# Six gate blocks of each MLP from seven block products, with a re-normed input and later splits

## The chip, the core and the metric

The kernel runs on one core of one Trainium2 chip. It is one program of five engines that run side by side and meet at semaphores: TensorE (PE in the profile; its weight loads are listed apart as PEld), VectorE (DVE), ScalarE (ACT), GpSimd (POOL) and SyncE (SP), which issues most of the DMAs. Operands live in SBUF and products are summed in PSUM, in banks of 128 partitions x 512 fp32. The metric is the device time of one execution in microseconds (us). The computation is in fp32, and every large matmul is made in parts, as told below.

## The reference

Two layers of a decoder trunk on 512 tokens (`S`), width 1024. Each layer has a mixer (attention and a short convolution in layer 0, gated linear attention in layer 1), the gated MLP that is changed here, and a per-layer embedding. The MLP:

```python
def _conv_ffn(h, w_up, conv_w, conv_b, w_down):
    u = _causal_depthwise_conv(h @ w_up, conv_w) + conv_b      # width 3, per column
    gate, up = jnp.split(u, 2, axis=-1)                        # 2816 columns each
    return (jax.nn.gelu(gate, approximate=False) * up) @ w_down
# in the trunk, for each layer i:
x = x + _conv_ffn(_rms_norm(x, ffn_norm[i]), ffn_w_up[i], ffn_conv_w[i], ffn_conv_b[i], ffn_w_down[i])
```

`_rms_norm` divides each token by the root of its mean square and multiplies by a gain per channel.

## The kernel before, in words

**Numbers.** An fp32 value is held as two fp32r parts, a high one and a low one (high: ScalarE rounds, L101 or L137; low: VectorE subtracts, L102 or L138). One product of two such pairs is three matmuls, `mm3` (L157 to L159): high x high, high x low, low x high. `split` makes the parts of an activation and `cut` (called by `weights`, after a DMA by SP into `raw`) those of a weight block, in two halves of 1024 elements a partition. `raw` has 2 buffers, `wh` and `wl` have 3 each.

**Layout.** The activations stand with channels in partitions and tokens in the free dimension: `xT[m]`, m = 0..7, are 128 channels x 512 tokens; `xg[m]` is the pair of parts of `xT[m]` times the gain, in the pools `a0` and `a1`. Weights are the stationary operand, 128 x 128 at a time.

**Up-projection (`ffn`).** A loop over d = 0..10 takes 256 columns of the gate and the 256 columns of the value that go with them; I call one turn a *pair* d. Each has two gate columns and two value columns of 128, in the order gate 0, value 0, gate 1, value 1. A column is 8 channel blocks (`ND`) x 3 = 24 matmuls of 512 tokens into one PSUM bank (`ps`, 4 banks; a second pool `pa` has 4 more). Behind each column stands `taps`: the sums are multiplied by `R`, the tokens' inverse root mean square spread over all partitions (L785, VectorE; the norm's factor is thus put behind the matmul), then the causal convolution: one tap with the bias on ScalarE (L786), two taps on VectorE (L788). The gate goes through Gelu (ScalarE, L810), the product of gate and value is made on VectorE (L813), and is split at once into `acts[f]`: the first 8 of the 22 into the pools `b0` and `b1` (8 buffers each), the others into tiles `four` (7 buffers).

**Down-projection.** `project` multiplies the 22 `acts` with `ffn_w_down`. In layer 0 the next norm follows, in layer 1 the seven-product embedding (`ple1`): it already replaces eight half-size block products by seven; its matmuls are recorded at L945 to L947 and are 512 wide, a few 256 wide. The gated linear attention of layer 1 has the lines L1344 (a matmul into one half of a `pa` tile) and L1351 (a copy out of the other half).

**Order.** A scheduler places the instructions of each engine; inside `manual_schedule` blocks the order of the engines named there is that of the program. A tile's buffer is used again when its readers are done, and an instruction waits for a whole tile, not for the part of it that it touches.

Of the kernel before, what the change touches and what calls it, by code (L numbers as in the profile page):

```python
# [18 lines left out]
P = 128  # L19
S = 512  # L20
D = 1024
NT = S // P
ND = D // P
DFF = 2816
NF = DFF // P
# [3 lines left out]
ET = mybir.EngineType  # L29
LEVELS = (64, 32, 16, 8, 4, 2, 1)  # L30
CW = 512
TWO_PI = 2.0 * np.pi
# [24 lines left out]
class Kernel:  # L57
# [711 lines left out]

    def ffn(self, i, next_gain):  # L770
        nc, a, tc = self.nc, self.a, self.tc
        xg, R = self.xg, None
        wu = a["ffn_w_up"][i].rearrange("(k p) n -> p k n", p=P)
        w0, w1, w2, bb = self.fcv
        with tc.tile_pool(name=f"ffn{i}", bufs=1) as fp:
            acts = [self.pair(self.fp, "b0", "b1") for f in range(8)]
            for f in range(8, NF, 2):
                four = self.four(fp)
                acts += [(four[:, 0], four[:, 1]), (four[:, 2], four[:, 3])]

            def taps(ps, f):
                y = fp.tile([P, S], F32, tag="zt", name=self.nm("zt"), bufs=4)
                z = fp.tile([P, S + 2], F32, tag="z", name=self.nm("z"), bufs=3)
                nc.gpsimd.memset(z[:, :2], 0.0)
                nc.vector.tensor_tensor(z[:, 2:], ps, R, ALU.mult)  # L785
                nc.scalar.activation(y, z[:, 2:], AF.Identity, scale=w2[:, f : f + 1], bias=bb[:, f : f + 1])  # L786
                for tap, w in ((1, w1), (0, w0)):
                    nc.vector.scalar_tensor_tensor(  # L788
                        out=y, in0=z[:, tap : tap + S], scalar=w[:, f : f + 1], in1=y, op0=ALU.mult, op1=ALU.add
                    )  # L790
                return y

            for d in range(NF // 2):
                wg = self.weights(wu[:, :, 256 * d : 256 * d + 256], ND, 256)
                wv = self.weights(wu[:, :, DFF + 256 * d : DFF + 256 * d + 256], ND, 256)
                for c in range(2):
                    f = 2 * d + c
                    got = []
                    pss = []
                    for w in (wg, wv):  # L800
                        ps = self.ps()
                        for k in range(ND):
                            self.mm3(ps, w(k, c * P, (c + 1) * P), xg[k], start=k == 0, stop=k == ND - 1)
                        pss.append(ps)
                    if R is None:
                        R = self.spread()
                    for w, ps, fo in ((wg, pss[0], f), (wv, pss[1], NF + f)):
                        y = taps(ps, fo)
                        if w is wg:
                            nc.scalar.activation(y, y, AF.Gelu)  # L810
                        got.append(y)
                    g, y = got
                    nc.vector.tensor_tensor(y, g, y, ALU.mult)  # L813
                    self.split(acts[f], y)
            self.begin_norm(("a0", "a1"))
            done = self.residual(next_gain)
            if i == 1:
                self.forms = []
                scratch = lambda: fp.tile([P, S], F32, tag="zt", name=self.nm("gx"), bufs=4)

                def done(m, ps):
                    nc.vector.tensor_tensor(self.xT[m], self.xT[m], ps, ALU.add)
                    self.blocks(m, next_gain, scratch)
# [75 lines left out]
    def ple1(self, fp):  # L899
# [49 lines left out]
        def back(hf, t):  # L949
# [6 lines left out]
            x = fp.tile([P, 512], F32, tag="zt", name=self.nm("xt"), bufs=4)  # L956
# [576 lines left out]
```

## Time and profile before

| | |
|---|---|
| time, median of 3 runs (lowest to highest) | 1247.71 us (1247.56 to 1248.11) |
| the profiled execution | 1248.2 us, of which its span in the trace is 1246.4 us |
| instructions | 15216 |
| TensorE / its weight loads, busy | 1236.1 us (99%) / 1023.9 us (82%) |
| VectorE / ScalarE / GpSimd, busy | 804.6 us (65%) / 561.5 us (45%) / 52.1 us (4%) |
| granted TensorE clock | 1.0 of full speed throughout |
| HBM read / written | 114.37 MB / 2.10 MB, 93 GB/s over the span |
| DMA of one `raw` of `ffn_w_up` (1024 KB) | 5.1 us from issue to landing |

The span is cut into engines' busy time; a group of instructions is given with its source line, its engine and operation, its output and inputs, its shape, its count, its total and mean time, and the idle time of the engine just before it with the instruction that ended it. Matmuls are pipelined: one of 512 columns is listed with about 390 ns from its start to its result, and the next starts sooner than that, so the pace is read from the distance between starts. A row of a timeline has the start in us, the duration in us, the engine and the operation; a bracket at its end is a wait and its releaser.

### The profile page before, as it was taken

The numbers are of one execution on the slowest core, as the hardware profiler recorded it, in microseconds if no ns is written. First come the engines' busy times: TensorE is split into PE (matmuls) and PEld (weight loads), VectorE is DVE, ScalarE is ACT, GpSimd is POOL, SyncE is SP. The second block draws the span as 40 slices with busy tenths as digits, with TensorE's granted clock in tenths as the row PEclk, the third lists the DMA queues.
The fourth block names the chain that finished last, engine by engine and source line by source line (L and its number), as shares of the span: only waits on it lengthen the run. The fifth ranks groups of instructions, "written<-read, shape, count | busy, mean of one in ns | idle before, by whom it ended". The sixth has DMA issues, their size and how long they took to land.

```text
span 1246.4 us, 15216 instructions
## 1 busy us (share of the span) xinstructions
PE 1236.1 (99%) x5984; PEld 1023.9 (82%) x5984; DVE 804.6 (65%) x1251; ACT 561.5 (45%) x873; POOL 52.1 (4%) x152
## 2 busy tenths in 40 slices
PE   9999999999999999999999999999999999999998
PEld 8877788888888888888987878888888888888887
DVE  6886556777777633346679875557777777444495
ACT  7466344444444322234563554335444444333374
POOL 2500000000000000000100000000000000000000
PEclk9999999999999999999999999999999999999999
DMA  6222232233333232223322222332223333322411
GB/s 214 92 80 56 83 102 83 88 100 102 101 102 101 83 103 93 93 74 103 111 91 68 69 68 68 101 110 95 83 94 102 101 101 102 101 93 94 149 46 68
DMA packets 111004, 117.45 MB, mean 94 GB/s; under 512 B 2728, under 2 KB 106210, under 8 KB 110932
## 3 DMA queue, kind: packets, MB, share of 16 engines
q1 hardware_dynamic: 109568, 115.35, 28.4%
q8 instruction: 47, 0.77, 0.2%
q0 software_dynamic: 560, 0.42, 0.2%
q10 hardware_dynamic: 804, 0.70, 0.2%
q14 instruction: 25, 0.20, 0.0%
HBM read 114.37 MB, written 2.10 MB: 93 GB/s over the span
## 4 chain that ended last, share of the span: by engine, by line
PE 88%; DVE 7%; ACT 2%; issue 1%; POOL 1%; DVEq 0%; ACTq 0%; POOLq 0%
PE ps L157 26%; PE ps L158 26%; PE ps L159 26%; DVE wl L138 1%; PE ps L947 1%; PE ps L946 1%; PE ps L945 1%; PE pa L1367 1%; PE pa L1344 0%; PE pa L595 0%; PE pa L158 0%; PE pa L192 0%; PE pa L159 0%; DVE F L1228 0%; PE pa L157 0%
## 5 line engine op out<-in xcount | busy, mean ns | idle before, releaser
L137 ACT ACTIVATE wh<-raw 128x1024 fp32r<-128x1024 f32 (+4 forms) x212 | 214.2, 1012 | 333.3 <-PE ps L158 298.7
L138 DVE TENSOR_TENSOR wl<-raw,wh 128x1024 fp32r<-128x1024 f32 (+4 forms) x212 | 246.5, 1164 | 153.2 <-ACT wh L137 152.1
L157 PE MATMUL ps<-a,wh 128*128 128x512 f32 x864 | 336.9, 390 | 0.0
L158 PE MATMUL ps<-a,wh 128*128 128x512 f32 x864 | 336.6, 390 | 0.0
L159 PE MATMUL ps<-a,wl 128*128 128x512 f32 x864 | 336.3, 389 | 0.0
L158 PEld LDWEIGHTS ps<-a,wh 128*128 128x128 f32 x864 | 162.3, 188 | 34.0 <-issue 0.3
L159 PEld LDWEIGHTS ps<-a,wl 128*128 128x128 f32 x864 | 162.2, 188 | 33.9
L157 PEld LDWEIGHTS ps<-a,wh 128*128 128x128 f32 x864 | 162.2, 188 | 33.7 <-issue 0.7
L788 DVE SCALAR_TENSOR_TENSOR zt<-z,vfa,zt 128x512 f32<-128x512 f32 x176 | 131.3, 749 | 3.6 <-ACT zt L786 0.6
L157 PE MATMUL ps<-b,wh 128*128 128x512 f32 x320 | 126.0, 395 | 0.5 <-ACT b L101 0.5
L159 PE MATMUL ps<-b,wl 128*128 128x512 f32 x320 | 125.7, 393 | 0.0
L158 PE MATMUL ps<-b,wh 128*128 128x512 f32 x320 | 125.0, 391 | 0.0
L785 DVE TENSOR_TENSOR z<-ps,R 128x512 f32<-128x512 f32 x88 | 60.3, 687 | 74.7 <-PE ps L159 74.7
L157 PE MATMUL ps<-four,wh 128*128 128x512 f32 x224 | 87.1, 389 | 0.0
L158 PE MATMUL ps<-four,wh 128*128 128x512 f32 x224 | 87.1, 389 | 0.0
L159 PE MATMUL ps<-four,wl 128*128 128x512 f32 x224 | 87.1, 389 | 0.0
L786 ACT ACTIVATE zt<-z,vfb 128x512 f32<-128x512 f32 x88 | 70.9, 808 | 5.0 <-DVE z L785 3.3
L157 PEld LDWEIGHTS ps<-b,wh 128*128 128x128 f32 x320 | 60.0, 188 | 14.0 <-ACT b L101 1.3
L159 PEld LDWEIGHTS ps<-b,wl 128*128 128x128 f32 x320 | 60.1, 188 | 12.5
L158 PEld LDWEIGHTS ps<-b,wh 128*128 128x128 f32 x320 | 60.1, 188 | 12.5
L810 ACT ACTIVATE zt<-zt 128x512 f32<-128x512 f32 x44 | 27.8, 631 | 74.9 <-DVE zt L788 74.8
L101 ACT ACTIVATE four<-zt 128x512 fp32r<-128x512 f32 x28 | 17.7, 632 | 77.3 <-DVE zt L813 77.3
(359 smaller groups left out, 1555.0 us busy)
## 6 DMA issues: line engine op xcount, KB each, us to landing
raw<-in_ffn_w_up_dram SPq DMA_DIRECT2D x44, 1024.0 KB, 5.1
raw<-in_ffn_w_down_dram SPq DMA_DIRECT2D x16, 1024.0 KB, 4.7
raw<-in_hy_w_in_dram SPq DMA_DIRECT2D x8, 1024.0 KB, 5.0
raw<-in_gla_w_in_dram SPq DMA_DIRECT2D x8, 1024.0 KB, 5.3
raw<-in_ffn_w_down_dram SPq DMA_DIRECT2D x8, 768.0 KB, 4.1
raw<-in_ple_w_gate_dram SPq DMA_DIRECT2D x6, 1024.0 KB, 4.7
raw<-in_gla_w_out_dram SPq DMA_DIRECT2D x4, 1024.0 KB, 4.8
raw<-in_gla_w_in_dram SPq DMA_DIRECT2D x4, 672.0 KB, 4.0
```

The lines of the kernel that those rows point to most:

```text
L101: nc.scalar.activation(h, src, AF.Copy)
L137: nc.scalar.activation(hv, v, AF.Copy)
L138: nc.vector.tensor_tensor(lv, v, hv.bitcast(F32), ALU.subtract)
L157: mm(out, lh, rh, start=start, stop=False)
L158: mm(out, lh, rl, start=False, stop=False)
L159: mm(out, ll, rh, start=False, stop=stop)
L785: nc.vector.tensor_tensor(z[:, 2:], ps, R, ALU.mult)
L786: nc.scalar.activation(y, z[:, 2:], AF.Identity, scale=w2[:, f : f + 1], bias=bb[:, f : f + 1])
L788: nc.vector.scalar_tensor_tensor(out=y, in0=z[:, tap : tap + S], scalar=w[:, f : f + 1], in1=y, op0=ALU.mult, op1=ALU.add)
L810: nc.scalar.activation(y, y, AF.Gelu)
L945: mm(o, lh, rh, start=first and j == 0, stop=False, **kw)
L946: mm(o, lh, rl, start=False, stop=False, **kw)
```

## The change

Three things, in both layers.

**Seven products.** For pairs d = 4 to 9 (`SEVEN = (4, 10)`) the two gate columns are not made as 2 x 8 channel blocks. The 8 channel blocks are taken as 4 couples (even block, odd block), the gate's columns as left and right 128, and the tokens as left and right 256. Each couple is then a 2 x 2 by 2 x 2 block product, made with seven block products instead of eight (Winograd's form). Of the weights, `seven` takes the blocks b11, b12 (even channels), b21, b22 (odd), cuts them into parts and makes differences between them on VectorE. Of the activations, `sums` makes four combinations per couple, s1 to s4, once per layer: in pairs d = 0 to 3, from the normed x (gain and `R` applied), split into parts in `b0` and `b1`.

In order of issue on TensorE, each product 4 couples x 3 = 12 matmuls of 256 tokens, 84 in all, into three banks, W (pool `pa`), X and Y (pool `ps`), by left and right half:

| | into | weights | activations | then, on ScalarE |
|---|---|---|---|---|
| P1 | W left, new | `w1`, first 128 | `xg` even, left | copied to Y left and to X left |
| P2 | W right, new | `w13`, first 128 | s1 | copied to `more` (SBUF) |
| P3 | Y left, added | `w2` | s2 | Y left copied to X right |
| P4 | X left, added | `w1`, second 128 | `xg` odd, left | |
| P5 | X right, added | `w13`, second 128 | s3 | X right copied to Y right |
| P6 | Y left, added | `w4`, second 128 | s4 | |
| P7 | X right, added | `w4`, first 128 | `xg` odd, right | |

X is then the first gate column; the second is Y plus `more` in both halves (VectorE). `w1`, `w13`, `w2`, `w4` are four cuts of the one `raw` tile, which VectorE changes between them: `w1` is cut from the blocks as loaded (b11 is its first 128, b21 its second); two subtractions follow and `w13` is cut from what then stands in b11 and b12; a third subtraction, and `w2` is cut (512 wide, into two tiles `t2`); a fourth, and `w4` is cut from b21 and b22. (In `ffn` the names `w0`, `w1`, `w2` mean the convolution's tap weights, as before.)

**Normed x.** From pair 4 on `xg` holds the normed x: at d = 4 the eight pairs are allocated anew in `a0` and `a1` and split from what `sums` left in `scratch`. `taps` then reads PSUM directly, with no multiplication by `R`. At d = 4 the value columns come first, at d = 5 to 9 the gate. Gelu (in pairs 4 to 9) and the product of gate and value (in all pairs) run on both columns of a pair at once, 1024 wide.

**Later splits.** The products stay in fp32 (`place`, `kept`) and are split later: the first 8 at the end of d = 9, into `b0` and `b1` (which the s1 to s4 have held until then), the others behind the loop, into `four` tiles.

The memset of two columns ahead of `z` goes with the padded form of the taps. In layer 1 the embedding takes its scratch halves from tiles of the new shape (`half`).

The diff, cut to its core:

```diff
+SEVEN = (4, 10)
+    def sums(self, j, gain, R, scratch):
+        nc = self.nc
+        H = S // 2
+        for u in range(2):
+            m = 2 * j + u
+            nc.vector.scalar_tensor_tensor(
+                out=scratch[:, u], in0=self.xT[m], scalar=gain[:, m : m + 1], in1=R, op0=ALU.mult, op1=ALU.mult
+            )
+        e, o, s12, s34 = (scratch[:, u] for u in range(4))
+        out = []
+        nc.vector.tensor_tensor(s12[:, :H], e[:, H:], o[:, H:], ALU.add)
+        nc.vector.tensor_tensor(s12[:, H:], s12[:, :H], e[:, :H], ALU.subtract)
+        nc.vector.tensor_tensor(s34[:, :H], e[:, :H], e[:, H:], ALU.subtract)
+        nc.vector.tensor_tensor(s34[:, H:], o[:, :H], s12[:, H:], ALU.subtract)
+        for x in (s12, s34):
+            hl = self.pair(self.fp, "b0", "b1")
+            self.split(hl, x)
+            for c in (slice(0, H), slice(H, S)):
+                out.append((hl[0][:, c], hl[1][:, c]))
+        return out
+    def seven(self, raw, xg, forms):
+        nc = self.nc
+        H = S // 2
+        mm = nc.tensor.matmul
+        W = self.pa()
+        X, Y = self.ps(), self.ps()
+        rv = raw.rearrange("p (j u) n -> p j u n", u=2)
+        def cut(src, wide=True):
+            if wide:
+                h, l = (self.wp.tile([P, 1024], F32R, tag=g, name=self.nm(g), bufs=3) for g in ("wh", "wl"))
+            else:
+                h, l = (self.sp.tile([P, S], F32R, tag="sq", name=self.nm("t2"), bufs=2) for _ in range(2))
+            h, l = (x.rearrange("p (j n) -> p j n", n=src.shape[2]) for x in (h, l))
+            nc.scalar.activation(h, src, AF.Copy)
+            nc.vector.tensor_tensor(l, src, h.bitcast(F32), ALU.subtract)
+            h, l = (x.rearrange("p j n -> p (j n)").rearrange("p (k n) -> p k n", n=P) for x in (h, l))
+            return lambda j, c: (h[:, (2 * j if wide else j) + c, :], l[:, (2 * j if wide else j) + c, :])
+        def product(out, w, c, x, first=False):
+            kw = dict(skip_group_check=True)
+            for j in range(ND // 2):
+                (wh, wl), (xh, xl) = w(j, c), x(j)
+                mm(out, wh, xh, start=first and j == 0, stop=False, **kw)
+                mm(out, wh, xl, start=False, stop=False, **kw)
+                mm(out, wl, xh, start=False, stop=j == ND // 2 - 1, **kw)
+        def plain(u, half):
+            c = slice(half * H, (half + 1) * H)
+            return lambda j: (xg[2 * j + u][0][:, c], xg[2 * j + u][1][:, c])
+        s1, s2, s3, s4 = (lambda j, q=q: forms[j][q] for q in range(4))
+        b11, b12, b21, b22 = (rv[:, :, u, c * P : (c + 1) * P] for u in range(2) for c in range(2))
+        left, right = slice(0, H), slice(H, S)
+        w1 = cut(raw[:, :, :P])
+        nc.vector.tensor_tensor(b11, b12, b11, ALU.subtract)
+        nc.vector.tensor_tensor(b12, b22, b12, ALU.subtract)
+        w13 = cut(rv[:, :, 0])
+        nc.vector.tensor_tensor(b11, b22, b11, ALU.subtract)
+        w2 = cut(b11, False)
+        nc.vector.tensor_tensor(b21, b21, b11, ALU.subtract)
+        w4 = cut(rv[:, :, 1])
+        with self.tc.manual_schedule(engines={ET.PE}):
+            product(W[:, left], w1, 0, plain(0, 0), True)
+            nc.scalar.copy(Y[:, left], W[:, left])
+            nc.scalar.copy(X[:, left], W[:, left])
+            product(W[:, right], w13, 0, s1, True)
+            more = self.sp.tile([P, S], F32, tag="acc", name=self.nm("more"), bufs=1)[:, :H]
+            nc.scalar.copy(more, W[:, right])
+            product(Y[:, left], w2, 0, s2)
+            nc.scalar.copy(X[:, right], Y[:, left])
+            product(X[:, left], w1, 1, plain(1, 0))
+            product(X[:, right], w13, 1, s3)
+            nc.scalar.copy(Y[:, right], X[:, right])
+            product(Y[:, left], w4, 1, s4)
+            product(X[:, right], w4, 0, plain(1, 1))
+        return X, Y, more
     def ffn(self, i, next_gain):
         nc, a, tc = self.nc, self.a, self.tc
         xg, R = self.xg, None
+        gain = self.g_ffn[i]
         wu = a["ffn_w_up"][i].rearrange("(k p) n -> p k n", p=P)
         w0, w1, w2, bb = self.fcv
         with tc.tile_pool(name=f"ffn{i}", bufs=1) as fp:
-            acts = [self.pair(self.fp, "b0", "b1") for f in range(8)]
-            for f in range(8, NF, 2):
+            forms, kept, acts = [], [], []
+            def both():
+                return fp.tile([P, 2, S], F32, tag="zt", name=self.nm("zt"), bufs=2)
+            def taps(y, ps, f, more=None, normed=True):
+                z = ps
+                if more is not None:
+                    z = fp.tile([P, S + 2], F32, tag="z", name=self.nm("z"), bufs=3)[:, :S]
+                    h2 = lambda x: x.rearrange("p (u t) -> p u t", u=2)
+                    nc.vector.tensor_tensor(
+                        h2(z), h2(ps), more.unsqueeze(1).to_broadcast([P, 2, S // 2]), ALU.add
+                    )
+                elif not normed:
+                    z = fp.tile([P, S + 2], F32, tag="z", name=self.nm("z"), bufs=3)[:, :S]
+                    nc.vector.tensor_tensor(z, ps, R, ALU.mult)
+                nc.scalar.activation(y, z, AF.Identity, scale=w2[:, f : f + 1], bias=bb[:, f : f + 1])
+                for tap, w in ((1, w1), (2, w0)):
+                    nc.vector.scalar_tensor_tensor(
+                        out=y[:, tap:], in0=z[:, : S - tap], scalar=w[:, f : f + 1], in1=y[:, tap:],
+                        op0=ALU.mult, op1=ALU.add,
+                    )
+            def columns(w, c, bank):
+                ps = bank()
+                for k in range(ND):
+                    self.mm3(ps, w(k, c * P, (c + 1) * P), xg[k], start=k == 0, stop=k == ND - 1)
+                return ps
+            def place(d):
+                if d == NF // 2 - 1:
+                    return None
+                if d % 2 == 0:
+                    kept.append(self.four(fp, F32))
+                return kept[d // 2][:, 2 * (d % 2) : 2 * (d % 2) + 2]
+            def split_pair(x):
                 four = self.four(fp)
-                acts += [(four[:, 0], four[:, 1]), (four[:, 2], four[:, 3])]
-
-            def taps(ps, f):
-                y = fp.tile([P, S], F32, tag="zt", name=self.nm("zt"), bufs=4)
-                z = fp.tile([P, S + 2], F32, tag="z", name=self.nm("z"), bufs=3)
-                nc.gpsimd.memset(z[:, :2], 0.0)
-                nc.vector.tensor_tensor(z[:, 2:], ps, R, ALU.mult)
-                nc.scalar.activation(y, z[:, 2:], AF.Identity, scale=w2[:, f : f + 1], bias=bb[:, f : f + 1])
-                for tap, w in ((1, w1), (0, w0)):
-                    nc.vector.scalar_tensor_tensor(
-                        out=y, in0=z[:, tap : tap + S], scalar=w[:, f : f + 1], in1=y, op0=ALU.mult, op1=ALU.add
-                    )
-                return y
-
+                self.split((four[:, :2], four[:, 2:]), x)
+                acts.extend([(four[:, u], four[:, 2 + u]) for u in range(2)])
+            def at(f):
+                return kept[f // 4][:, f % 4]
+            scratch = [self.four(fp, F32) for _ in range(ND // 2)]
             for d in range(NF // 2):
-                wg = self.weights(wu[:, :, 256 * d : 256 * d + 256], ND, 256)
-                wv = self.weights(wu[:, :, DFF + 256 * d : DFF + 256 * d + 256], ND, 256)
-                for c in range(2):
-                    f = 2 * d + c
-                    got = []
-                    pss = []
-                    for w in (wg, wv):
-                        ps = self.ps()
-                        for k in range(ND):
-                            self.mm3(ps, w(k, c * P, (c + 1) * P), xg[k], start=k == 0, stop=k == ND - 1)
-                        pss.append(ps)
-                    if R is None:
-                        R = self.spread()
-                    for w, ps, fo in ((wg, pss[0], f), (wv, pss[1], NF + f)):
-                        y = taps(ps, fo)
-                        if w is wg:
-                            nc.scalar.activation(y, y, AF.Gelu)
-                        got.append(y)
-                    g, y = got
-                    nc.vector.tensor_tensor(y, g, y, ALU.mult)
-                    self.split(acts[f], y)
+                g, y = both(), both()
+                normed = d >= SEVEN[0]
+                if d == SEVEN[0]:
+                    xg = []
+                    for m in range(ND):
+                        xg.append(self.pair(self.fp, "a0", "a1"))
+                        self.split(xg[m], scratch[m // 2][:, m % 2])
+                cg, cv = 256 * d, DFF + 256 * d
+                if SEVEN[0] <= d < SEVEN[1]:
+                    def value():
+                        wv = self.weights(wu[:, :, cv : cv + 256], ND, 256)
+                        for c in range(2):
+                            taps(y[:, c], columns(wv, c, self.pa), NF + 2 * d + c)
+                    def gate():
+                        raw = self.raw(ND, 256)
+                        nc.sync.dma_start(raw, wu[:, :, cg : cg + 256])
+                        X, Y, more = self.seven(raw, xg, forms)
+                        taps(g[:, 0], X, 2 * d)
+                        taps(g[:, 1], Y, 2 * d + 1, more)
+                        nc.scalar.activation(g, g, AF.Gelu)
+                    for half in (value, gate) if d == SEVEN[0] else (gate, value):
+                        half()
+                else:
+                    wg = self.weights(wu[:, :, cg : cg + 256], ND, 256)
+                    wv = self.weights(wu[:, :, cv : cv + 256], ND, 256)
+                    for c in range(2):
+                        pss = [columns(w, c, self.ps) for w in (wg, wv)]
+                        if R is None:
+                            R = self.spread()
+                        taps(g[:, c], pss[0], 2 * d + c, None, normed)
+                        nc.scalar.activation(g[:, c], g[:, c], AF.Gelu)
+                        taps(y[:, c], pss[1], NF + 2 * d + c, None, normed)
+                u = place(d)
+                if u is None:
+                    u = y
+                nc.vector.tensor_tensor(u, g, y, ALU.mult)
+                if d < ND // 2:
+                    forms.append(self.sums(d, gain, R, scratch[d]))
+                if d == SEVEN[1] - 1:
+                    for f in range(8):
+                        hl = self.pair(self.fp, "b0", "b1")
+                        self.split(hl, at(f))
+                        acts.append(hl)
+            for d in range(4, NF // 2):
+                split_pair(y if d == NF // 2 - 1 else kept[d // 2][:, 2 * (d % 2) : 2 * (d % 2) + 2])
             self.begin_norm(("a0", "a1"))
             done = self.residual(next_gain)
             if i == 1:
                 self.forms = []
-                scratch = lambda: fp.tile([P, S], F32, tag="zt", name=self.nm("gx"), bufs=4)
+                halves = []
+                def half():
+                    if not halves:
+                        x = both()
+                        halves.extend([x[:, 0], x[:, 1]])
+                    return halves.pop(0)
...
-            x = fp.tile([P, 512], F32, tag="zt", name=self.nm("xt"), bufs=4)
+            x = self.half()
```

More of the change, by code (lines that the diff above doesn't have):

```diff
@@ L818, in ffn @@
                 self.forms = []
[L819 removed]
+                halves = []
[4 more added lines that the diff above has]
+                    return halves.pop(0)
+                self.half = half
                 def done(m, ps):
                     nc.vector.tensor_tensor(self.xT[m], self.xT[m], ps, ALU.add)
[L823 removed]
+                    self.blocks(m, next_gain, half)
             self.project(self.rows(a["ffn_w_down"][i]), acts, ND, done)
```

## The prediction

> **What bounds the kernel now.** I read the page's busy shares first, then the busy time in the up-projection, its groups of instructions, and two pieces of timeline that price what the change adds.
>
> The page, parts 1 and 4:
>
> ```profile
> PE 1236.1 (99%) x5984; PEld 1023.9 (82%) x5984; DVE 804.6 (65%) x1251; ACT 561.5 (45%) x873; POOL 52.1 (4%) x152
> ...
> PE 88%; DVE 7%; ACT 2%; issue 1%; POOL 1%; DVEq 0%; ACTq 0%; POOLq 0%
> ```
>
> TensorE is the bound. The windows (span, then busy us of PE, PEld, DVE, ACT, POOL, clock, DMA share) show the first up-projection without its first two columns of output:
>
> ```profile
> 196.60:424.90 228.30, 228.30 (x1009) 189.02 (x1008) 168.68 (x213) 105.63 (x130) 4.08 (x41) 1.00 0.30 96
> ```
>
> 228.3 us for 1008 matmuls is 0.2264 each: no stall at all, so whatever TensorE is made to wait is added in full. VectorE has 60 us of 228 free. Its groups and ScalarE's in that window (mean ns before the bar's end):
>
> ```profile
> L788 DVE SCALAR_TENSOR_TENSOR zt<-z,vfa,zt 128x512 f32<-128x512 f32 x86 | 64.2, 749 | 1.8 <-ACT zt L786 0.3
> ...
> L138 DVE TENSOR_TENSOR wl<-raw,wh 128x1024 fp32r<-128x1024 f32 x42 | 51.4, 1225 | 9.2 <-ACT wh L137 8.7
> L137 ACT ACTIVATE wh<-raw 128x1024 fp32r<-128x1024 f32 x42 | 44.6, 1062 | 31.4 <-PE ps L158 31.2
> L786 ACT ACTIVATE zt<-z,vfb 128x512 f32<-128x512 f32 x43 | 34.7, 808 | 2.5 <-DVE z L785 1.7
> L785 DVE TENSOR_TENSOR z<-ps,R 128x512 f32<-128x512 f32 x43 | 29.5, 687 | 35.5 <-PE ps L159 35.5
> L813 DVE TENSOR_TENSOR zt<-zt,zt 128x512 f32<-128x512 f32 x21 | 14.5, 692 | 1.3 <-ACT zt L810 0.6
> ```
>
> The nearest rows for the new 256-column products are at the end of the second embedding (timeline of PE):
>
> ```profile
> 1239.08 0.39 PE L159 MATMUL pa<-wh,four 128*128 128x512 f32 x1
> 1239.30 0.28 PE L945 MATMUL ps<-wh,a 128*128 128x256 f32 x1
> ...
> 1242.06 0.28 PE L947 MATMUL ps<-four,b 128*128 128x256 f32 x1
> ```
>
> 24 of them stand between 1239.30 and 1242.06, so 2.76/23 = 0.120 each, 0.28 from start to result; weight loads (188 ns each) do not hold them.
>
> For a copy out of one half of a bank while the other half is wanted, the gated linear attention has the pattern:
>
> ```profile
> 752.05 0.37 ACT L1351 COPY st<-pa 128x256 f32<-128x256 f32 x1
> ...
> 752.47 0.30 PEld L1344 LDWEIGHTS pa<-vt,F 128*128 128x128 f32 x2 [0.38 <-ACT st L1351]
> ```
>
> L1351 copies one half of a `pa` tile; the matmul into its other half starts 0.05 after the copy's end. Elsewhere a restarted fp32r stream loses another 0.11 because the next weights were not loaded (gaps of 335 instead of 227 ns, at 619.05 and 1206.74).
>
> **The change, part by part.** Per gate, 48 x 0.2264 = 10.87 becomes 84 x 0.120 = 10.08: 0.79 saved, **9.4 us** for twelve gates. Everything else must hide beside that.
>
> Call the products P1 to P7 in order of issue (1.44 us each). W, X and Y are one bank each, and in the built program waits go by the whole tile. P2 (right half of W) waits for both copies of W's left half. P4 (left half of X) waits for the copy of Y into X's right half, made after P3. P6 waits for the copy of X into Y, made after P5. Bare prices: P2: 0.28 to P1's result, 0.09 to ScalarE's start (seen at L137), two copies of 0.375, 0.05 back, 0.11 restart, less the 0.12 pitch: 1.13. P4, one copy: 0.77. P6 is covered by value matmuls that the scheduler put ahead of it (five, in pairs 5 to 8), but the third of those needs the VectorE half of a weight cut whose ScalarE half may start only when P4 has read `w1`: 0.37 + 1.06 + 0.03 + 1.22 + 0.05 after P4's eleventh matmul, 0.6 to 0.7 after its turn.
>
> The Trainium skill (PSUM — Partial Sum Buffer, summary rules) says to read PSUM beside a running matmul from another bank and to guard by bank. The L1351 row agrees; if halves were free, P2 and P4 would not wait and the sum would be some 23 us less.
>
> VectorE's chain is longer still. Pairs 6 to 8, from P6's result: `more` added (0.04 + 0.69), bias step (0.84), four tap steps (3.0), next `w1` low part (1.22), two subtractions (1.38), two value taps (1.5), `w13` low part (1.22), two subtractions (1.38): 11.3. Then ScalarE: `w4` high part (1.06), the last value column's bias step (0.81), two copies (0.75), with lags 2.75: P2 can start 14.1 after P6's result. P6 to its result is 1.6, so 15.7; TensorE has only P6, P7, 43 value matmuls and P1 = 14.05 for it. P2's stall is 1.65 instead of 1.13. Pair total: 20.95 of matmuls + 1.65 + 0.77 + 0.7 + restarts 0.1 = 24.17 against 21.73 now: **+2.44 each, +7.3 for three**. The durations of steps that before doesn't show are bounded by a 512-wide copy (0.58) and a 128-wide activation (0.28) for the 256-wide copies; L1351's 0.375 has their size and source. Taps from PSUM: 0.745 at L105, as from SBUF.
>
> Pair 3 to 4: the eight normed `xg` pairs go into the buffers of the old ones, so they are cut while the last column of pair 3 runs. In the built order VectorE has in pair 3 the sums of pairs 2 and 3 (2 x 4.6), its usual 14.6 and these eight low parts (5.5) ahead of the weights of pair 4's second column: about 33 us from 21.5 before the boundary. I add them along the queue: the first `xg` low part ends 1.4 after the boundary, the eighth 10.4, the weight cut 11.6. The second column so ends at 16.75 instead of 11.1: **+5.6**.
>
> Gate 4: P2 1.15, P3 0.9 (low part of `w2` behind taps of the value columns), P4 0.78, P6 0.55 (two foreign matmuls only): 3.4 - 0.79 = **+2.6**. Pair 5's gate follows at once: P2 1.25; P3 waits for ScalarE's high part of `w2` behind the 1024-wide Gelu and then its low part behind the product, 3.4; P4 0.8; value cut 0.7: 6.2 - 0.79 = **+5.4**.
>
> Pair 9: splits of the first activations stand in ScalarE's queue between the copies, so P2 1.7, P4 1.4, P6 1.1: **+3.5** after the saving.
>
> Off the path: pairs 0 to 3 get 4.6 of sums each, 19.2 of VectorE in 21.7, four PSUM banks of slack; dropping `R` saves 28 x 0.69 of VectorE a layer; GpSimd's `z` memsets vanish; weight DMAs keep their number, 5.1 us, and are issued as buffers come free, well ahead of the cuts. The later splits (8 x 0.69 and 7 x 1.22 on VectorE, 14 a layer) lie in pairs 9 and 10, where VectorE's queue ends about 5 us ahead of each weight's use; I cost them at nothing, and at up to 14 a layer if that cover is gone.
>
> Sum per layer 13.6 + 7.3 + 3.5 = 24.4, the same order in both layers: +48.8. On the profiled execution, 1248.2 (span 1246.4, 1.8 around it): 1297.0. The median of the runs is 0.5 below the profiled one: **1296.5 us**.
>
> **Rivals.**
> - *Faster: the waits are covered and the arithmetic counts.* One mechanism: the copies run beside the other half's matmuls, and value matmuls fill the rest; then 1247.7 - 9.4 = 1238.3. It decides where a gate's stalls fall under 0.79 us. For it: VectorE and ScalarE are idle 26% and 54% of that window. Against: one copy alone costs P4 0.77, and P2 waits for two. 4%; break-even within 0.2%: 2%.
> - *Bank waits only.* VectorE's chain is absorbed: 12 x (1.13 + 0.77) + 8 x 0.7 + 2 x 5.6 - 9.4 = +30, 1278. For it: the chain misses by only half a microsecond per pair. Against: the gaps of pairs 4, 5 and 9 come from fixed queue order. 20%.
> - *Splits uncovered.* VectorE, at 17.5 of 24 us in pairs 6 to 8 and full in 3 and 9, runs late into the down-projection: +28, 1325. Against: `four` tiles are wanted only 10.9 us into it. 8%.
> - *Weight loads bound the narrow products*, so the product count doesn't fall in time: 84 x (0.188 - 0.120) = 5.7 a gate more, +69 on top: 1365. The 0.120 rows speak against it. 3%.
>
> By the Trainium skill (TensorE: Matmul & The Clock Gate, LDWEIGHTS) a load of 128 columns is estimated at 128/1.2 = 107 ns, under the 0.120 pitch.
>
> **How the numbers follow.** Forecast 63%, the rivals 4, 2, 20, 8 and 3%. Range: from 1270 (bank waits with a shorter restart) to 1314 (chain steps 10% longer, +1.5 in eight gaps, and 3 more at each boundary); it leaves out both ends' rivals, under 2 in 10. A measurement can tell about 0.2%, 2.5 us. Faster 0.04, same 0.02, slower 0.94.
>
> **What would show it.** After: 256-column matmuls at 0.120 inside a product; PE idle before P2 of 1.1 to 1.7 us put down to ScalarE's copy of W, 0.8 before P4 to the copy of Y; PE waiting for `a` tiles on VectorE at the boundary of pairs 3 and 4, some 5 us a layer; up-projections of about 261 instead of 236 us, down-projections unchanged. If P2 and P4 start without a gap, the bank reading is wrong; if the gaps of pair 6 equal those bare prices, the chain is.

## The result

The changed kernel takes 1285.32 us (median of 6; five of them between 1282.27 and 1285.53), before 1247.63 us: a ratio of 1.0295, 95% interval 1.0281 to 1.0309. Slower was forecast, 1296.5 us with a range of 1270 to 1314. The profile that came with this result is of the sixth execution, which took 2610.42 us, with 512-wide matmuls 0.45 us apart (median) instead of 0.227 at a listed clock of 1.00; the lines of the changed kernel below are from its second run, e1, whose profiled span is 1280.5 us.

The page of e1, parts 1 and 4:

```profile
PE 1240.9 (97%) x6416; PEld 1037.6 (81%) x6416; DVE 856.9 (67%) x1323; ACT 603.4 (47%) x963; POOL 44.2 (3%) x64
...
PE 71%; DVE 18%; ACT 6%; issue 3%; POOL 1%; DMA 0%; ACTq 0%; DVEq 0%; POOLq 0%
```

TensorE has 432 matmuls more (twelve gates of 84 instead of 48), and it was busy 99% of the span before; now TensorE holds 71% of the chain that ended last, where it held 88% before, and other engines hold a quarter. The windows (span, then busy us of PE, PEld, DVE, ACT, POOL, clock, DMA share, GB/s) of layer 1 from the third column of the up-projection to the first matmul with a `four` tile:

```profile
857.17:1112.68 255.51, 241.19 (x1273) 204.82 (x1272) 200.71 (x256) 129.97 (x180) 0.00 (x0) 1.00 0.28 90
```

The same stretch of before is 239.36 us long (839.30 to 1078.66), with TensorE busy in all of it. So a layer loses 16.15 us here; layer 0 loses 17.4. The down-projections behind it keep their pace: 29.92 us from one `four` group to the next, before and after. These two stretches hold 33.5 of the 34.1 us by which the spans differ.

Who TensorE waits for in that stretch of layer 1 (engine, line, waited for: us in total, times, longest). L821 to L823 are the matmuls of the products; L845 is the second copy of W, L850 that of Y into X, L853 that of X into Y, L812 and L813 the cuts in `seven`; L103 is the low part of `split`, L139 that of `cut`:

```profile
PE pa L821 <- ACT ps L845: 4.7, 6, 0.8
PE ps L821 <- ACT ps L850: 3.3, 6, 0.8
PE ps L821 <- ACT t L812: 1.9, 1, 1.9
PE pa L160 <- DVE wl L139: 1.9, 5, 0.4
PE ps L823 <- DVE t L813: 1.1, 2, 0.8
PE pa L159 <- DVE a L103: 0.8, 1, 0.8
PE ps L821 <- ACT ps L853: 0.6, 2, 0.3
```

In order: P2 in all six gates, P4 in all six, P3 once (pair 5, 1.9), the third matmul of the value column (pairs 5 to 8, and a weight cut at the boundary), `w2`'s low part (pairs 4 and 5), the boundary of pairs 3 and 4, and P6 in pairs 4 and 9. This view counts idle time from a modelled end; from start to start, less the usual 0.120 or 0.226, the losses of one layer are (my sums over the trace):

| place | forecast | measured |
|---|---|---|
| boundary of pairs 3 and 4 | 5.6 | 2.1 |
| gate of pair 4 | 3.4 | 2.7 |
| pair 5 | 6.2 | 5.7 |
| pairs 6, 7 and 8, each | 3.2 | 2.5 |
| pair 9 | 4.3 | 2.7 |
| six gates' saving | -4.7 | -4.9 |
| sum | 24.4 | 15.8, and 0.4 that I can't place |

The forecast column is the prediction's, with the saving taken out of each row again.

### The profile page after: what moved, and what is told of

The parts are those of the page before. It is cut to its first block, busy times and chain, and to the rows that moved or that the text cites. A ratio compares the mean times of both kernels' runs of the same rounds, so it can differ in the third digit from the quotient of the medians.

```text
span 2608.6 us, 16085 instructions
## 1 busy us (share of the span) xinstructions
PE 2583.0 (99%) x6416; PEld 1748.5 (67%) x6416; DVE 865.6 (33%) x1323; ACT 619.0 (24%) x963; POOL 43.0 (2%) x64
## 4 chain that ended last, share of the span: by engine, by line
PE 99%; ACT 1%; DVE 0%; issue 0%; ACTq 0%
PE ps L158 23%; PE ps L159 23%; PE ps L160 22%; PE pa L159 4%; PE pa L160 4%; PE pa L158 4%; PE ps L821 2%; PE ps L823 2%; PE ps L822 2%; PE pa L821 1%; PE ps L1100 1%; PE ps L1099 1%; PE ps L1101 1%; PE pa L822 1%; PE pa L823 1%; PE pa L596 1%
## 5 line engine op out<-in xcount | busy, mean ns | idle before, releaser
L139 DVE TENSOR_TENSOR wl<-raw,wh 128x1024 fp32r<-128x1024 f32 (+4 forms) x188 | 217.7, 1158 | 572.8 <-ACT wh L138 570.7
L158 PE MATMUL ps<-b,wh 128*128 128x512 f32 x320 | 227.5, 712 | 0.4 <-ACT b L102 0.4
L160 PE MATMUL ps<-b,wl 128*128 128x512 f32 x320 | 227.7, 712 | 0.0
L159 PE MATMUL ps<-b,wh 128*128 128x512 f32 x320 | 226.4, 708 | 0.0
L158 PE MATMUL ps<-four,wh 128*128 128x512 f32 x224 | 151.1, 675 | 0.0
L160 PE MATMUL ps<-four,wl 128*128 128x512 f32 x224 | 151.1, 675 | 0.0
L159 PE MATMUL ps<-four,wh 128*128 128x512 f32 x224 | 150.9, 674 | 0.0
L159 PEld LDWEIGHTS ps<-b,wh 128*128 128x128 f32 x320 | 98.9, 309 | 58.7 <-issue 55.6
L160 PEld LDWEIGHTS ps<-b,wl 128*128 128x128 f32 x320 | 99.1, 310 | 58.3 <-issue 55.1
L158 PEld LDWEIGHTS ps<-b,wh 128*128 128x128 f32 x320 | 97.3, 305 | 60.3 <-issue 54.1
L160 PE MATMUL pa<-a,wl 128*128 128x512 f32 x192 | 129.1, 675 | 0.0
L158 PE MATMUL pa<-a,wh 128*128 128x512 f32 x192 | 129.0, 674 | 0.0
L159 PE MATMUL pa<-a,wh 128*128 128x512 f32 x192 | 128.5, 669 | 0.0
L158 PEld LDWEIGHTS ps<-four,wh 128*128 128x128 f32 x224 | 67.0, 299 | 38.0 <-issue 35.4
L160 PEld LDWEIGHTS ps<-four,wl 128*128 128x128 f32 x224 | 66.7, 298 | 38.3 <-issue 35.7
```

The lines of the kernel that those rows point to most:

```text
L139: nc.vector.tensor_tensor(lv, v, hv.bitcast(F32), ALU.subtract)
L158: mm(out, lh, rh, start=start, stop=False)
L159: mm(out, lh, rl, start=False, stop=False)
L160: mm(out, ll, rh, start=False, stop=stop)
```

## The experiments

**e1, the changed kernel again.** No edit.

> The changed kernel itself once more, for a trace in which TensorE runs at its usual pace. Known: 1285 us, so 37.7 over before, 47 us of stalls if the 9.4 of saved matmuls came. Theory of the prediction (VectorE's chain): PE idle before P2 1.65 and before P4 0.77 in pairs 6 to 8, 0.6 to 0.7 before the third value matmul, 5.6 a layer at the boundary of pairs 3 and 4, 4.9 of gaps more in pair 5 than in pairs 6 to 8. Rival (bank waits only): P2 1.13 and P4 0.77 in every gate, 5.6 at the boundary, nothing else over 0.5. Rival (weight loads): 256-wide matmuls 0.188 apart instead of 0.120.

Measured: 1283.7 us, ratio 1.0290 (1.0273 to 1.0308). In pairs 6 to 8 the gap is 0.96 before P2 and 0.66 before P4, each with 0.10 more at the matmul behind it (the restart), and 0.55 + 0.11 before the third value matmul. 256-wide matmuls start 0.120 apart. That is what bank waits and the buffer of `w1` give: 1.06, 0.76, 0.66 against bare prices of 1.13, 0.77 and 0.6 to 0.7. The timeline of pair 7 of layer 0 around P2 (start in us, duration in us), ScalarE's and TensorE's rows:

```profile
349.85 1.06 ACT L812 ACTIVATE wh<-raw 128x1024 fp32r<-128x1024 f32 x1 [0.15 <-DVE raw L840]
350.81 0.76 ACT L881 ACTIVATE zt<-pa,vfb 128x512 f32<-128x512 f32 x1
...
351.07 0.28 PE L823 MATMUL pa<-a,wl 128*128 128x256 f32 x1
351.47 0.37 ACT L844 COPY ps<-pa 128x256 f32<-128x256 f32 x1
351.78 0.34 ACT L845 COPY ps<-pa 128x256 f32<-128x256 f32 x1
...
352.17 0.39 PE L821 MATMUL pa<-b,wh 128*128 128x256 f32 x1 [0.81 <-ACT ps L845]
```

P1's last matmul starts at 351.07 and its result is there at 351.35; the first copy starts 0.12 later, the second ends at 352.12, P2 starts at 352.17. VectorE's chain ends at about the same moment: the cut of `w4` (L812) waits for VectorE's subtraction (L840), the value column's bias step (L881) follows it at once, and the copy starts 0.66 after that, as soon as ScalarE gets to it. In pairs 4 and 5 no such chain stands ahead, the copy starts 0.04 after P1's result, and the gap is 0.88. So in pairs 6 to 9 the chain is worth at most 0.09, where the prediction had it worth 0.5.

**e2, everything but the seven products.** The gates of pairs 4 to 9 are plain columns again; sums, re-split, taps without `R` and later splits stay.

```diff
-                        X, Y, more = self.seven(raw, xg, forms)
-                        taps(g[:, 0], X, 2 * d)
-                        taps(g[:, 1], Y, 2 * d + 1, more)
+                        wg = self.weights(wu[:, :, cg : cg + 256], ND, 256)
+                        for c in range(2):
+                            taps(g[:, c], columns(wg, c, self.ps), 2 * d + c)
```

> The changed kernel with the twelve gates of pairs 4 to 9 made as plain columns of 24 matmuls again; the four sums, the re-split of the normed x, taps without R and the later splits stay. Theory of the prediction: only the boundary of pairs 3 and 4 is left, 2 x 5.6, so 1259 us, with no gap at a gate. Rival (splits uncovered): the later splits run into the down-projection, up to 1287. Rival (boundary free): 1248.

Measured: 1252.1 us, ratio 1.0034 (1.0020 to 1.0047). TensorE's waits from 190 to 460 us, the whole up-projection of layer 0:

```profile
PE pa L159 <- DVE a L103: 0.7, 1, 0.7
PE pa L160 <- DVE wl L139: 0.4, 1, 0.4
```

Only the boundary is left, 1.85 us with its restarts; twice that is 3.7 of the 4 us. The later splits cost nothing: their cover held, and "splits uncovered" is out. The boundary is real, at a third of its forecast.

**e3, P2 in a bank of its own.**

```diff
-        W = self.pa()
+        W, W2 = self.pa(), self.pa()
-            product(W[:, right], w13, 0, s1, True)
+            product(W2[:, left], w13, 0, s1, True)
-            nc.scalar.copy(more, W[:, right])
+            nc.scalar.copy(more, W2[:, left])
```

> The changed kernel with P2 in a bank of its own (a second pa tile) instead of the right half of W. Theory of the prediction: P2 loses its wait for the two copies of W, and P3 waits for what is left of them after P2's 1.44: 0.2 in pairs 6 to 8; 12 x about 1.2 = 14 us less than the changed kernel, 1271. Rival (VectorE's low part of w13 is what P2 waits for): less than 3 us gained, the gap stays before P2 and is put down to VectorE.

Measured: 1276.6 us, ratio 1.0232 (1.0217 to 1.0247): 7 less than e1, half of what I expected. TensorE's waits in pairs 6 to 9 of layer 0:

```profile
PE ps L821 <- ACT ps L850: 2.5, 4, 1.0
PE pa L160 <- DVE wl L139: 1.1, 3, 0.4
```

P2's wait is gone and P3 has none: a pair of 6 to 8 takes 22.41 us where e1's takes 23.48. So the shared bank was P2's whole price there, and VectorE has the low part of `w13` ready in time. The gain was given back in pairs 4 and 5, where P3 waits for the cut of `w2` and TensorE now only reaches that wait earlier: in pair 4, P3 has 0.45 and 0.86 where e1 has 0.43, and in pair 5 its gap grows from 2.10 to 2.84 and a stretch at half clock follows (below).

**e4, no normed x.** `sums` multiplies by the gain alone, `xg` is not split anew, and `taps` multiplies each column by `R` again.

```diff
-            nc.vector.scalar_tensor_tensor(
-                out=scratch[:, u], in0=self.xT[m], scalar=gain[:, m : m + 1], in1=R, op0=ALU.mult, op1=ALU.mult
-            )
+            nc.vector.tensor_scalar(scratch[:, u], self.xT[m], gain[:, m : m + 1], None, op0=ALU.mult)
...
+                    nc.vector.tensor_tensor(z, z, R, ALU.mult)
...
-                normed = d >= SEVEN[0]
-                if d == SEVEN[0]:
-                    xg = []
-                    for m in range(ND):
-                        xg.append(self.pair(self.fp, "a0", "a1"))
-                        self.split(xg[m], scratch[m // 2][:, m % 2])
+                normed = False
```

> The changed kernel without the normed x: the four sums are made from gain times x, xg is not split anew at pair 4, and R is multiplied behind each column as before (4 x 0.69 more on VectorE in each of the pairs 4 to 10, 8 low and 8 high parts fewer at the boundary). Theory of the prediction: the boundary's 2 x 5.6 go, but in pairs 5 to 9 VectorE's chain is 2.7 longer each and P2 waits for it: +27 for ten, 1301. Rival (bank waits only, VectorE has room): 1274.

Measured: 1305.3 us, ratio 1.0459 (1.0444 to 1.0475). The boundary's gaps are gone. In pairs 6 to 9 of layer 1:

```profile
PE pa L819 <- ACT ps L843: 11.6, 4, 2.9
PE ps L819 <- ACT ps L848: 2.0, 4, 0.5
PE pa L160 <- DVE wl L139: 1.1, 3, 0.4
```

P2's gap is now 3.07 instead of 0.97 in every one of them, still put down to the copy, since the copy stands in ScalarE's queue behind what VectorE releases late. Four more multiplications, which start 0.61 us apart, lengthen the chain by 2.4; P2 came 2.1 later. So the chain exists, and 2.4 us more of it reach P2 nearly whole. The two figures can't be set against each other to a tenth, since ScalarE's order changed too: the value column's bias step and the cuts of `w2` and `w4` now stand between the two copies (995.89 and 998.35).

**e8, from pair 5 on.** The changed kernel with one constant changed: `SEVEN = (5, 10)`.

> The changed kernel with only SEVEN = (5, 10) for (4, 10): pair 4 as before the change, the normed x split anew at pair 5. Theory (boundary stall from the sums in VectorE's queue): 2 x 2.1 gone, and two gates at 1.7 each: 1284 - 4.2 - 3.4 = 1276. Rival (the re-split itself is too slow for the matmuls that follow): only the gates' 3.4 go, 1280.

Measured: 1275.2 us, ratio 1.0220 (1.0204 to 1.0235), 1276 expected. TensorE waits for no `a` tile at all; the first gap of layer 0 over 0.08 stands before P2 of pair 5. The same re-split, one pair after the last `sums`, is free. The boundary's stall is the backlog of the sums in VectorE's queue, as forecast; and P3's 2.10 is now in pair 6, again the gate that follows another gate at once.

**e5 and e6, w1 in a buffer of its own, and P4 ahead of P3.** e5 is e3 with the parts of `w1` in a new tile `four` for each gate; e6 also issues P4 before P3 (the last part of the diff).

```diff
+            if own:
+                four = self.four(fp).rearrange("p a b -> p (a b)")
+                h, l = four[:, :1024], four[:, 1024:]
...
-        w1 = cut(raw[:, :, :P])
+        w1 = cut(raw[:, :, :P], own=True)
...
+            product(X[:, left], w1, 1, plain(1, 0))
             product(Y[:, left], w2, 0, s2)
             nc.scalar.copy(X[:, right], Y[:, left])
-            product(X[:, left], w1, 1, plain(1, 0))
```

> The two-bank kernel (e3) with the cut of w1 in a buffer of its own (a free tile four) instead of in the ring of three that the value columns' cuts share. Theory (the value cut waits for P4 to have read w1): the wait before the third value matmul, 0.66 with its restart in each of pairs 5 to 8, goes; 8 x 0.66 = 5 us off, 1271. Rival (VectorE is late with the value cut anyway): the gap stays, 1276.

> e5 with P4 issued ahead of P3. Theory (P4 waits only because the copy of Y into X's right half is issued before it): P4's 0.76 goes in all twelve gates; the same copy is now awaited by P5, where two or three value matmuls (0.45 to 0.68) stand in the built order, so about 0.3 is left: 12 x 0.45 = 5 us off e5, 1266. Rival (the wait only moves to P5): same as e5, 1271.

Measured: 1315.2 us (ratio 1.0543, 1.0527 to 1.0558) and 1312.1 us (1.0516, 1.0500 to 1.0531); nothing that either theory had. The largest waits of e5 from 965 to 1110 us, and ScalarE's timeline ahead of the first of them:

```profile
PE pa L824 <- ACT four L815: 8.8, 3, 5.1
PE pa L826 <- DVE four L816: 5.7, 3, 2.5
```

```profile
979.68 1.06 ACT L937 ACTIVATE zt<-zt 128x1024 f32<-128x1024 f32 x1 [2.19 <-DVE zt L886]
980.64 1.04 ACT L815 ACTIVATE four<-raw 128x1024 fp32r<-128x1024 f32 x1
```

The cut of `w1` (L815), which P1 needs, stands in ScalarE's queue right behind the 1024-wide Gelu (L937) of the gate before, and its low part behind the product on VectorE. P1 waits 5.3 us for it. The cut shows no wait of its own behind Gelu; what it lost is its place in the queue. The value column's wait for VectorE's cut, 0.55 in e3, is not among e5's waits any more. In e6 no wait for the copy of Y is left before P4.

**e11, one tile for w1.** e5 with one tile `four` that stays `w1`'s. The expectation calls it e6, but in the kernel that ran P3 stands ahead of P4, as in e5 and e3, so it is compared with these.

> e6 (two banks, P4 ahead of P3, seven products in pairs 4 to 9, gate first) with w1's parts in one tile four that is kept for w1, instead of a new one for each pair. In the built order ScalarE's cut of w1 now stands ahead of the taps of the gate before and of the long Gelu. Theory (e5 and e6 lost 29 and 26 us a layer because w1's cut, in a new tile each pair, was placed behind Gelu, product and taps in the queues): the gaps of 2 to 5 us before P1 go; left are the boundary's 2.1 and pair 5's 3 to 4 a layer, and 0.3 to 0.6 a gate: 1255 to 1262. Rival (two gates in a row leave VectorE too little time wherever w1 lies): over 1285.

Measured: 1263.3 us, ratio 1.0126 (1.0109 to 1.0142): 52 less than e5, and 13 less than e3, from which it differs by `w1`'s tile alone. In the built order the cut of `w1` is back ahead of Gelu and taps. That the place of the cut cost e5 its time is shown (e6 has the same waits before P1); why the scheduler places it so when each gate has a new tile was not tried. In layer 1, pairs 6 to 9 have no gap over 0.2. P4's wait is gone there without P4 being moved: the value column's cuts are ready sooner, and three of its matmuls stand between P3 and P4 (1001.20 to 1001.90 in pair 7), where e3 had none. The boundary (2.1), pair 4 (2.7) and pair 5 (P3: 2.84 and 0.89, with matmuls at half clock behind them) are what is left. What P4 ahead of P3 is worth by itself was not run with `w1` in its place.

**e7, value columns first, seven products from pair 5.** e6 with `SEVEN = (5, 10)` and `for half in (value, gate)` in all of these pairs.

> e6 with seven products in pairs 5 to 9 only (pair 4 as before the change, R behind it), the normed x split anew at pair 5, and the value columns ahead of the gate in all of these pairs, so no two gates follow each other. Theory (the boundary's 2.1 come from the sums of pairs 2 and 3 in VectorE's queue, and the 4 us in pair 5 from two gates in a row): both go, 2 x 6 off less one gate's saving: e6 less 11, 1255. Rival (the re-split alone stalls TensorE): 2 x 2 stay, 1259. Half-speed stretches behind long gaps should go too.

Measured: 1256.4 us, ratio 1.0069 (1.0052 to 1.0086). Boundary and P3's wait are both gone, as expected: no two gates follow each other, and the re-split has no sums ahead of it. That the number came out is in part luck: 1255 was counted from the 1266 expected of e6, which took 1312. With the value columns between two gates the waits for `w1` before P1 are gone as well, though each gate still has a new tile. Pairs 7 and 9 have gaps of 0.55 and 1.41, and of 1.18 and 1.14, before and in P2: the two parts of `w13` stand behind the second value column's bias step on ScalarE and its taps on VectorE.

**e9, the cuts written ahead.** e7 with the gate's cuts and subtractions ahead of the value columns in the program, and one tile for `w1`; which of the two did it was not separated. `seven` now stops in the middle: the first `next(run)` makes the four cuts and the subtractions, the second the products.

```diff
+        yield
...
+        yield X, Y, more
...
+                    wv = self.weights(wu[:, :, cv : cv + 256], ND, 256)
+                    raw = self.raw(ND, 256)
+                    nc.sync.dma_start(raw, wu[:, :, cg : cg + 256])
+                    run = self.seven(raw, xg, forms, own)
+                    next(run)
+                    for c in range(2):
+                        taps(y[:, c], columns(wv, c, self.pa), NF + 2 * d + c)
+                    X, Y, more = next(run)
...
```

> e7 with the gate's cuts and subtractions written ahead of the value columns' taps (so that VectorE makes the low part of w13 before the second value column's taps), and w1 in one tile four that stays w1's. Theory (e7's gaps of 0.6 to 1.4 before and in P2 of pairs 7 and 9 come from VectorE's queue order): they go, and 0.24 before P5 and before P6 are left: ten gates at 0.81 saved and 0.48 lost, 1248 - 3 = 1245, perhaps 1 more for pair 9. Rival (VectorE has too little time in any order): 1252 to 1256 as e7.

Measured: 1245.36 us, ratio 0.9982 (0.9973 to 0.9990). It is the one version that is faster than the kernel before, by 2.4 us between the medians. Layer 1, the stretch shown above:

```profile
837.46:1075.12 237.66, 237.64 (x1237) 202.58 (x1236) 196.18 (x253) 126.76 (x174) 0.00 (x0) 1.00 0.30 97
```

237.66 against 239.36, 1.70 less: five gates save 0.81 each, 4.05, and 2.0 of it goes in gaps of 0.06 to 0.20 with their restarts, most of them before P5 and P6; 0.35 I can't place.

**e10, the gaps filled by hand.** Four matmuls of the next pair's first value column are written ahead of P5 and five ahead of P6 (`FILL = (4, 5)`).

```diff
             nc.scalar.copy(X[:, right], Y[:, left])
+            fill(FILL[0])
             product(X[:, right], w13, 1, s3)
             nc.scalar.copy(Y[:, right], X[:, right])
+            fill(FILL[1])
```

> e9 with the first value column of the next pair written into the gate's order on TensorE: four of its matmuls ahead of P5, five ahead of P6, those with the high part of the weights first. Theory (the waits before P5 and P6 are the copy between the halves, 0.28 + 0.09 + 0.37 + 0.05, and 0.9 to 1.1 us of other matmuls cover it): no gap in the ten gates, 1248 - 8 = 1240, up to 1242 with pair 9. Rival (the filling column waits for its bank, whose taps VectorE makes late): gaps of about 0.5 in front of the fill, 1245.

Measured: 1248.1 us, ratio 1.0003 (0.9994 to 1.0012); a miss. Some gaps before P5 and P6 stayed (0.08 to 0.35 in layer 1, and the restart), and new ones came, 0.97 before P4 of pair 6 and 0.85 in pair 10, where a copy and a cut stand later in ScalarE's queue: 3.7 a layer against e9's 2.0. ScalarE's rows for the copies ahead of P5 (L856) and of P6 (L859) in pair 7 of layer 1:

```profile
997.36 0.36 ACT L856 COPY ps<-ps 128x256 f32<-128x256 f32 x1 [2.51 <-PE ps L825]
...
999.59 1.06 ACT L139 ACTIVATE wh<-raw 128x1024 fp32r<-128x1024 f32 x1 [0.84 <-PE ps L824]
1000.55 0.37 ACT L859 COPY ps<-ps 128x256 f32<-128x256 f32 x1
```

The first copy starts 0.04 after P3's result, four matmuls cover it, and P5 has no gap; so it is in eight of the ten gates. The second stands behind the cut of the next weights and starts 0.88 after P5's result (999.67), and six matmuls don't cover that. The two gaps left before P5, both in pair 8, stand behind a cut as well, that of `w1`. The theory took the copy for the price; what is left is the place of the copy in ScalarE's queue. It was so in e9, where the built order already had two to four value matmuls ahead of P5 and six ahead of P6, so the filling by hand had little to add. A kernel with these copies ahead of the cuts was not run.

## Why the prediction was right, and where it was off

The sign, the mechanism and the places were right. TensorE had no slack, so each wait counts in full (33.5 of 34.1 us lie in the two up-projections); the saving is 0.81 a gate (0.79 forecast); P2 waits for two copies (e3), P4 for one, the third value matmul for the buffer of `w1` (e11), each within 0.1 of its bare price; the boundary waits for the sums in VectorE's queue (e2, e8); two gates in a row stall P3 for `w2` (e8 moves it to pair 6, and with the value columns first, in e7, it is gone); the later splits are free (e2). The rival "faster" fell with the first copy: a gate lost over twice what it saved. "Weight loads" fell with the 0.120.

The size was off. By spans, 1246.4 + 48.8 = 1295.2 was forecast and e1 has 1280.5. By the sign that the prediction itself named, the gaps of pair 6 at the bare prices, what it had wrong is the chain on VectorE and ScalarE. A good part of that is one kind of term: these chains were summed from durations. Two rows of VectorE in the trace of before, and three of e1:

```profile
224.89 1.23 DVE L138 TENSOR_TENSOR wl<-raw,wh 128x1024 fp32r<-128x1024 f32 x1
226.03 1.53 DVE L788 SCALAR_TENSOR_TENSOR zt<-z,vfa,zt 128x512 f32<-128x512 f32 x2
```

```profile
340.40 0.75 DVE L883 SCALAR_TENSOR_TENSOR zt<-z,vfa,zt 128x511 f32<-128x511 f32 x1 [0.88 <-ACT zt L881]
341.07 0.75 DVE L883 SCALAR_TENSOR_TENSOR zt<-ps,vfa,zt 128x511 f32<-128x511 f32 x1
341.74 0.74 DVE L883 SCALAR_TENSOR_TENSOR zt<-z,vfa,zt 128x510 f32<-128x510 f32 x1
```

An instruction listed with 1.23 is followed 1.14 later, one with 0.75 is followed 0.67 later: the next starts before the listed end. I had used starts for TensorE and durations for the other two. In pairs 6 to 8 it is 13.35 us from the first step behind P6's result, the add of `more` (338.82), to P2 (352.17), where I had 14.1. With that the chain ends at the bank wait, at most 0.09 behind it (e1), and "P2 1.65" should have been its bare price; e1 has 1.07.

At the boundary the spacing is half of it. I had the first low part of the new `xg` end 1.4 us after the boundary; it ended 4.6 before it (271.5, the first new matmul near 276.1), and the eighth at 279.5 where I had 286.5. The prediction gave VectorE about 33 us of work from 21.5 before the boundary to the second column's weight cut, but the terms that it lists for that (2 x 4.6, 14.6 and 5.5) add up to 29.3. In e1 this stretch, 254.6 to 280.6, holds 29.2 us of listed durations and takes 26.0: the 3.2 are 0.08 on each of some forty instructions, and the rest was never in the terms.

Those two places, 0.7 in each of three pairs and 3.5 at the boundary, are 5.6 of the 8.6 a layer; pair 9, where I let the splits stand between the copies, is 1.6 more (P2 there has 0.97 like the others). Three sums of the prediction are off by little: the parts of P2's bare price add up to 1.16 and not 1.13, those of P4's to 0.785 and not 0.77, and pair 9's to 3.4 and not 3.5.

So the measured time lies between two of the stated cases, nearer to "bank waits only" (1278) in what it is made of: P2 and P4 at their bare prices, next to no chain. That rival's 1278 is near for the wrong parts: it lacks P3's waits in pairs 4 and 5 (0.5 and 3.3 a layer) and has the boundary 3.5 a layer too dear.

On the rule of the Trainium skill that was weighed (PSUM — Partial Sum Buffer, summary rules: read from another bank): e3 agrees, and shows what the bank apart is worth, 1.07 a gate where nothing else is late. The wait is one that the program makes for the whole tile; what a read beside a write in one bank would do on the chip, no run here shows.

## What to carry to other kernels

A saving on a full engine is worth what the other engines can feed: price each new wait from its own rows before counting matmuls, and then write the order so that the feeding work stands early in its queues. Sum a chain on VectorE or ScalarE from start to start, and check the spacing on two rows that stand back to back; some forty instructions at 0.08 too much made a chain 3.2 us too long. A buffer of its own is worth nothing if the instruction that fills it is placed behind a long one: `w1`'s cost 39 us so (e5 against e3), and gained 13 where the cut kept its place (e11). Where a gap stays before a copy's reader, look at what stands ahead of the copy in its queue before covering it with other work (e10).

## What the runs showed of the hardware

Long gaps cost more than themselves. In layer 0 and in layer 1 of e1 the same gaps stand in pair 5 (2.10, and 1.00 two matmuls later); the 4 us behind the first, in both layers:

```profile
304.20:308.20 4.00, 2.56 (x12) 2.06 (x12) 2.57 (x3) 1.39 (x3) 0.00 (x0) 0.76 0.06 10
965.07:969.07 4.00, 2.52 (x16) 2.11 (x17) 2.56 (x3) 1.39 (x3) 0.00 (x0) 1.00 0.09 10
```

The clock is 0.76 in the one and 1.00 in the other, with 12 matmuls instead of 16; ten of layer 0's stand 0.21 apart instead of 0.12, and that layer's up-projection is 1.2 us longer. In e4, behind each gap of 3.07:

```profile
999.00:1003.00 4.00, 4.00 (x22) 4.00 (x22) 2.44 (x3) 0.37 (x1) 0.00 (x0) 0.57 0.36 105
```

the stretch at half pace lasts from 999.2 to 1002.6, 3.4 us, and costs about 1.5 us. It came in e7 behind gaps of no more than 0.55 and 1.41 (pair 7), and in pair 9 behind 1.18 and 1.15 in layer 0, but not behind 1.18 and 1.14 in layer 1. The Trainium skill (TensorE: Matmul & The Clock Gate, Part 1: The HAM clock gate) has a free-running window of about 3.4 us, after an idle one of which TensorE runs at half clock. The length agrees, and so does it that the same gaps do it in one layer and not in the other; that the window must be idle altogether doesn't: the longest of these gaps is 3.07, so 3.4 us hold matmuls. I had no term for it. The five executions of the result range over 3 us, with a mean clock of 0.994 (1285.5 us) to 0.999 (1282.3 us); before's six range over 1.
